# Attention on one core: pair 1 handled by head, score buffers in one PSUM tile, five double-width exponentials, and the order of the work as a table

## The chip, the cores and the metric

The kernel runs on one core of one Trainium2 chip. The metric is device time in microseconds (us); lower is better. A core has a matrix engine (TensorE, PE in the profile; its weight loads are PEld), VectorE (DVE), ScalarE (ACT), GpSimd (POOL) and SyncE (SP), which here only issues transfers. Each engine works through its own queue in order, and a queue waits on semaphores that the others raise. Matrix results land in PSUM, which TensorE writes and VectorE and ScalarE read; everything else lies in SBUF.

## The reference

```python
scores = np.einsum('bhqd,bhkd->bhqk', q, k) * scale       # scale = 1/8
attn = np.exp(scores - scores.max(axis=-1, keepdims=True))
attn = attn / attn.sum(axis=-1, keepdims=True)
return np.einsum('bhqk,bhkd->bhqd', attn, v)
```

q, k and v are float32 of shape 8 x 8 x 512 x 64: 64 heads of 512 positions and 64 features.

## The kernel before

The 64 heads make 32 **pairs** g of two heads (h = 0, 1, called a and b). SyncE loads k, q and v of a pair in 256 KB each (line 509). GpSimd rounds them to float16 (casts: k and q at line 525, v at line 515). TensorE turns k and q so that features lie on partitions (line 558, eight 128x128 transposes for a pair), and VectorE copies the result from PSUM to SBUF (`tqk`, line 571). Scores come transposed, keys on partitions: a **block** is 128 keys by 512 queries, and two blocks make a **group** m, one PSUM buffer of 1024 columns and two banks (`st`). There are three such buffers, used in turn, so the scores of group m (line 598) need the reader of group m-3 to be done. A head's features fill 64 partitions, so the two blocks of a group run side by side on the two halves of the array. The groups are numbered 0 to 128; 127 and 128 are two halves of the last one.

112 groups go to ScalarE: one exponential of 1024 columns each (line 602), from `st` to a float16 tile `pt` (24 of them). The other 16, listed in `Plan.ON_DVE`, go to VectorE, which makes the exponential from bits: a **raise** that reads the buffer (line 625), then five **passes** on SBUF: two scalings (lines 642 and 651), a product (659), a scaling (661) and a product (665). Such a group leaves two tiles, `pe` and `pd`, whose sum is the exponential, so TensorE multiplies twice for it. Then the values (line 704): a **unit** is 128 queries of a head, four or more matmuls of 65 columns, the 65th giving the row's sum. Seven units fill a bank of PSUM; VectorE takes the reciprocals (line 671) and multiplies (line 676) into `ring`, from which SyncE stores heads (line 694). Two more PSUM banks (`x0`, `x1`) serve transposes and values in turn.

Pair 0 is written out by hand (`first_pair`, with its exponentials at line 801). Pair 1 comes next: k and q are loaded in 256 KB each, k is rounded by GpSimd whole, q half by VectorE (line 523) and half by GpSimd (line 524), and it is turned and copied in two parts, k of both heads first and then q of both heads (line 565).

The order of everything else is made by `Plan`: it steps through time with a cost for each operation and writes down, for each engine, what comes when (`step_pe`, `step_dve`, `step_pool`, `step_sp`). Scores go ahead of other work on TensorE when two buffers are free or ScalarE is about to run dry. Casts can be tied behind a VectorE instruction (`cast_behind`), because GpSimd and VectorE share a way to SBUF. The end is written apart: head b of the last pair is multiplied in four parts as its last exponentials come (line 720), normalised (lines 733 and 734) and stored (line 740).

Of the kernel before, what the change touches and what calls it, by code (L numbers as in the profile page):

```python
# [17 lines left out]
class Plan:  # L18

    SLOT, EXP, EXP_DONE, EXP_FIXED = 216, 853, 181, 64  # L20
    INTO, OUT_OF = 96, 96
    TRANSPOSE, V_UNIT = 222, 128
    TO_ACT, TO_DVE, TO_PE = 220, 210, 60

    COPY, NORM, RAISE = (601, 690), (50, 133), (1132, 1215)
    RECIPROCAL = 115
    SCALE, PRODUCT, EXTRA = 333, 600, 29
    COPY_1 = (400, 190)
    NORM_COLUMN, PASS_DONE = 67, 115
    PASSES = (SCALE, SCALE, PRODUCT, SCALE, PRODUCT)  # L30
    BITS = 2
    NEEDS = (None, None, 0, 2, 3)
    FIRST_EXP = 5000
    STEP = 5
    CALM, KEEN = 9000, 4
    FIRST_UNIT = 4
    KNOWN, OVER = (13, 15, 18, 20, 22, 24, 27, 42, 50, 61, 69, 97), 6
    ON_DVE = (5, 10, 16, 25, 28, 39, 44, 54, 63, 66, 74, 81, 91, 96, 103, 116)

    LATE_NORM, LATE_COPY, HURRY, SOON, BACKLOG = 700, 1500, 800, 160, 600  # L40
    LATE_MUL, WAIT = 400, 200
    SLACK, AHEAD = 0, 2

    CAST, CAST_PORT, CAST_DONE, TO_POOL = 557, 475, 130, 150
    SCALE_PORT, PRODUCT_PORT, GAP, REACH = 271, 537, 20, 5
    FIRST_LAND, LOAD, STORE, LATENCY, ISSUE = 5200, 752, 376, 2300, 470
    QUEUED, URGENT = 3500, 16
    PAIRED, STORE_ISSUE = 18, 520
    RAW, QK16, NV, NU = 7, 5, 12, 112
    PAIR, DUEK, DUEV, DUEL, PRE = 3300, 3550, 6000, 5000, 0  # L50

    def __init__(self, groups, pairs, first):
        self.groups, self.pairs = groups, pairs
        self.pe, self.act, self.dve = 7000, self.FIRST_EXP, 6300
        self.pool, self.port, self.dma = 4600, 4600, self.FIRST_LAND
        self.m, self.tiled = first, True
        self.read = []
        self.exps = {}
        for m in range(first):
            self.act += self.EXP + self.EXP_FIXED  # L60
            self.exps[m] = self.act + self.EXP_DONE
            self.read.append(self.exps[m])
        self.tq = {0: 5800}
        self.transposed = {0: 5800}
        self.next_t = 1
        self.part_t = 0
        self.banks = [5100, 5800]
        self.todo = [(g, h) for g in range(pairs) for h in range(2)]
        self.last = self.todo.pop()
        self.last_part = 0  # L70
        self.head = None
        self.units = self.FIRST_UNIT
        self.member = {b: m for m, grp in enumerate(groups) for b in grp}
        self.ready = []
        self.passes = []
        self.passed = {}
        self.raised = set()
        self.steps = []
        self.busy_dve = 0
        self.order, self.paired = [], 0  # L80

        late = {grp[0][0] for m, grp in enumerate(groups) if m in self.ON_DVE}
        due = []
        for g in range(pairs):
            scores = 5000 + self.PAIR * g
            if g:
                due += [(scores - self.DUEK, g, "k"), (scores - self.DUEK + 10, g, "q")]
            due.append((scores + self.DUEV + (self.DUEL if g in late else 0), g, "v"))
        self.due = sorted(due)
        self.uncast = list(self.due)  # L90
        self.casts = []
        self.landed, self.cast_done = {}, {}
        self.first_loads = [(g, n) for _, g, n in self.due if g < self.RAW]
        self.first_loads += [(self.RAW, "k"), (self.RAW, "q")]
        for x in self.first_loads:
            self.dma += self.LOAD
            self.landed[x] = self.dma
        self.loads, self.stores, self.stored = [], [], []
        self.sp = 1650 + 470 * len(self.first_loads)

    def note(self, t, *what):
        self.steps.append((t, len(self.steps)) + what)

    def trigger(self, t):

        ops = self.ops
        if not ops or ops[-1][1] <= t - 300:  # L110
            return 1, None
        n = len(ops) - 1
        while (
            n > 0
            and len(ops) - n < self.REACH
            and not ops[n][2]
            and ops[n][0] - ops[n - 1][1] <= self.GAP
        ):
            n -= 1
        if n > 0 and ops[n][0] - ops[n - 1][1] <= self.GAP:  # L120
            n -= 1
        return len(ops) - n, ops[n][1]

    def emit(self, t, back, after):
        _, g, n = self.uncast.pop(0)
        shared = (g, n) == (1, "q")
        self.note(t, "cast", g, n, back if t > self.CALM else 0)
        if not shared:
            self.casts.append((g, n, t if after is None else after + self.TO_POOL))
        if g + self.RAW < self.pairs:  # L130
            self.loads.append((g + self.RAW, n))

    def fits(self, t, soon=0):
        if not self.uncast:
            return False
        _, g, n = self.uncast[0]
        if n != "v" and g >= self.QK16 and self.transposed.get(g - self.QK16, 1e9) > t:
            return False
        return self.landed.get((g, n), 1e9) <= t + soon

    def step_pool(self, t):
        if self.uncast and self.uncast[0][1:] != (1, "q") and not self.casts and self.pool <= t:
            quiet = not self.passes and self.port <= t and not any(x[1] == "raise" for x in self.ready)
            if self.fits(t) and (quiet or self.uncast[0][0] - self.PRE < t):
                self.emit(t, 1, None)
        if self.casts and self.pool <= t and self.port <= t:
            g, n, after = self.casts[0]
            if after <= t and self.landed.get((g, n), 1e9) <= t:
                self.casts.pop(0)
                begin = max(self.pool, self.port, after, self.landed[(g, n)])  # L150
                self.pool = begin + self.CAST
                self.port = begin + self.CAST_PORT
                self.cast_done[(g, n)] = begin + self.CAST + self.CAST_DONE

    def step_sp(self, t):
        if self.sp > t or (self.loads and self.dma > t + self.QUEUED):
            return
        urgent = len(self.stores) > self.URGENT
        if self.loads and not urgent:
            g, n = self.loads[0]  # L160
            if self.cast_done.get((g - self.RAW, n), 1e9) <= t:
                self.loads.pop(0)
                self.note(t, "load", g, n)
                self.dma = max(self.dma, t + self.LATENCY - self.LOAD) + self.LOAD
                self.landed[(g, n)] = self.dma
                self.sp = t + self.ISSUE
                return
        if self.stores and self.stores[0] <= t:
            both = self.both()
            if both and (len(self.stores) < 2 or self.stores[1] > t):  # L170
                return
            heads = 2 if both else 1
            self.note(t, "store", heads)
            self.dma = max(self.dma, t + self.LATENCY - heads * self.STORE) + heads * self.STORE
            for _ in range(heads):
                self.stores.pop(0)
                self.stored.append(self.dma)
            self.paired += heads - 1
            self.sp = t + self.STORE_ISSUE

    def both(self):

        n = len(self.stored)
        g, h, u = self.order[n]
        return (
            self.paired < self.PAIRED
            and g < self.pairs - 2
            and h == 0
            and n + 1 < len(self.order)
            and self.order[n + 1][0] == g  # L190
            and u % self.NU + 8 <= self.NU
        )

    def room(self, t, u):
        heads = (u - self.NU - self.FIRST_UNIT + 3) // 4
        return heads <= 0 or len(self.stored) >= heads and self.stored[heads - 1] <= t

    def free(self, n=0):
        m = self.m + n
        if m >= len(self.groups):  # L200
            return 1e9
        g = self.groups[m][0][0]
        return max(0 if m < 3 else self.read[m - 3], self.tq.get(g, 1e9))

    def for_dve(self, m):
        return m in self.ON_DVE
# [692 lines left out]
```

## Time and profile before

| | us |
|---|---|
| median of 3 runs | 113.66 (113.52 to 114.11) |
| the profiled execution | 113.92 |
| its span, first to last instruction | 112.1 |
| first exponential starts / last one ends | 5.20 / 108.49 |
| ACT busy | 105.5 (94%) |
| PE busy | 103.2 (92%) |
| DVE busy | 100.8 (90%) |
| POOL busy | 65.9 (59%) |

What lies around the span, 1.8 us, is time before the first and after the last instruction. The page also gives the busy share in 40 slices of 2.8 us, the chain of work that ended last, and groups of instructions with their idle time. One thing is needed to read them: an instruction's recorded time goes from its start to its last write, and the next one on the same engine may start before that. So the distance from start to start is what an instruction costs its engine, not the recorded duration, and a small wait can be hidden in the overlap without any idle time being shown.

### The profile page before, as it was taken

The numbers are of one execution on the slowest core, as the hardware profiler recorded it, in microseconds if no ns is written. First come the engines' busy times: TensorE is split into PE (matmuls) and PEld (weight loads), VectorE is DVE, ScalarE is ACT, GpSimd is POOL, SyncE is SP. The second block draws the span as 40 slices with busy tenths as digits, with TensorE's granted clock in tenths as the row PEclk, the third lists the DMA queues.
The fourth block names the chain that finished last, engine by engine and source line by source line (L and its number), as shares of the span: only waits on it lengthen the run. The fifth ranks groups of instructions, "written<-read, shape, count | busy, mean of one in ns | idle before, by whom it ended". The sixth has DMA issues, their size and how long they took to land.

```text
span 112.1 us, 4408 instructions
## 1 busy us (share of the span) xinstructions
PE 103.2 (92%) x1728; PEld 69.4 (62%) x1728; DVE 100.8 (90%) x227; ACT 105.5 (94%) x118; POOL 65.9 (59%) x127
## 2 busy tenths in 40 slices
PE   7978889999799998999989999899999999999980
PEld 7634555766367766658647767577557577675660
DVE  1647999999999999999999999999999999997390
ACT  4599999999999999999999999999999999999970
POOL 2147768549756886495594786876784855600000
PEclk9999999999999999999999999999999999999997
DMA  3999999999999999999999999999999974142354
GB/s 106 276 359 353 345 350 347 355 336 349 345 347 336 341 346 343 354 364 375 370 358 382 350 355 377 354 372 362 343 366 305 349 245 143 52 141 99 97 167 161
DMA packets 35093, 33.84 MB, mean 302 GB/s; under 512 B 2304, under 2 KB 35072, under 8 KB 35072
## 3 DMA queue, kind: packets, MB, share of 16 engines
q1 hardware_dynamic: 34496, 33.04, 90.4%
q10 hardware_dynamic: 576, 0.52, 1.4%
q8 instruction: 13, 0.21, 0.8%
q14 instruction: 8, 0.07, 0.2%
HBM read 25.17 MB, written 8.39 MB: 299 GB/s over the span
## 4 chain that ended last, share of the span: by engine, by line
DVE 39%; PE 24%; DMA 15%; issue 8%; POOL 7%; SPq 3%; ACT 2%; POOLq 0%; ACTq 0%
PE o L704 13%; DMA v<-in_v_dram 10%; PE st L598 8%; DVE pd L625 8%; DVE tqk L571 7%; DVE ring L676 7%; DMA q<-in_q_dram 5%; DVE m L659 4%; POOL qkp L525 4%; DVE pd L665 4%; POOL vp L515 3%; PE tp L558 2%; SPq L509 2%; DVE m L642 2%; DVE pe L651 2%
## 5 line engine op out<-in xcount | busy, mean ns | idle before, releaser
L602 ACT ACTIVATE pt<-st 128x1024 f16<-128x1024 f32 (+1 forms) x110 | 100.3, 1144 | 0.2 <-PE st L598 0.2
L704 PEld LDWEIGHTS <-pt 128*128 128x128 f16 x880 | 38.8, 98 | 12.1 <-issue 10.2
L704 PE MATMUL o<-vp,pt 128*128 128x65 f16 x880 | 45.3, 194 | 0.4 <-POOL vp L515 0.2
L598 PE MATMUL st<-tqk 64*128 64x512 f16 (+1 forms) x250 | 41.7, 380 | 2.6 <-ACT pt L602 1.4
L525 POOL CAST qkp<-k 128x512 f16<-128x512 f32 x31 | 22.2, 717 | 11.3 <-DVE rc L671 5.3
L525 POOL CAST qkp<-q 128x512 f16<-128x512 f32 x30 | 21.7, 725 | 9.0 <-DVE rc L671 5.3
L515 POOL CAST vp<-v 128x512 f16<-128x512 f32 x32 | 21.4, 679 | 9.2 <-PE st L598 2.4
L676 DVE TENSOR_TENSOR ring<-o,rc 128x448 f32<-128x448 f32 (+2 forms) x37 | 22.3, 606 | 0.4
L704 PE MATMUL o<-vp,pe 128*128 128x65 f16 x128 | 21.8, 194 | 0.0
L704 PE MATMUL o<-vp,pd 128*128 128x65 f16 x128 | 21.7, 192 | 0.0
L558 PE MATMUL tp<-ident,qkp 128*128 128x128 f16 x248 | 19.6, 220 | 1.6 <-DVE tqk L571 0.8
L558 PEld LDWEIGHTS <-qkp 128*128 128x128 f16 x248 | 14.4, 97 | 9.9 <-issue 4.6
L571 DVE COPY tqk<-tp 128x1024 f16<-128x1024 f16 x30 | 20.3, 683 | 0.0
L625 DVE TENSOR_SCALAR pd<-st 128x1024 uint16<-128x1024 f32 x16 | 19.5, 1216 | 0.7 <-PE st L598 0.7
L598 PEld LDWEIGHTS <-tqk 64*128 64x128 f16 x250 | 10.7, 93 | 11.8 <-issue 4.6
L704 PEld LDWEIGHTS <-pe 128*128 128x128 f16 x128 | 12.5, 98 | 3.4 <-issue 3.3
L704 PEld LDWEIGHTS <-pd 128*128 128x128 f16 x128 | 12.5, 98 | 0.0
L659 DVE TENSOR_TENSOR m<-m 128x1024 f16<-128x1024 f16 x16 | 11.0, 685 | 0.0
L665 DVE TENSOR_TENSOR pd<-pd,m 128x1024 f16<-128x1024 f16 x16 | 10.9, 684 | 0.0
L671 DVE RECIPROCAL rc<-o 128x7 f32<-128x7 f32 (+2 forms) x37 | 7.4, 199 | 2.6 <-PE o L704 2.4
L661 DVE TENSOR_SCALAR m<-m 128x1024 f16<-128x1024 f16 x16 | 6.7, 418 | 0.1
L651 DVE TENSOR_SCALAR pe<-pd 128x1024 uint16<-128x1024 uint16 x16 | 6.6, 411 | 0.0
(51 smaller groups left out, 34.9 us busy)
## 6 DMA issues: line engine op xcount, KB each, us to landing
v<-in_v_dram SPq DMA_DIRECT2D x32, 256.0 KB, 5.8
k<-in_k_dram SPq DMA_DIRECT2D x31, 256.0 KB, 5.8
q<-in_q_dram SPq DMA_DIRECT2D x31, 256.0 KB, 5.9
out_dram<-ring SPq DMA_DIRECT2D x18, 256.0 KB, 5.5
out_dram<-ring SPq DMA_DIRECT2D x25, 128.0 KB, 2.2
k<-in_k_dram ACTq DMA_DIRECT2D x2, 128.0 KB, 2.8
q<-in_q_dram SPq DMA_DIRECT2D x2, 128.0 KB, 2.6
out_dram<-ring ACTq DMA_DIRECT2D x2, 128.0 KB, 1.9
```

Of the source, the lines that this page charges most:

```text
L515: return nc.gpsimd.tensor_copy(out=vps[g % NV][:, :, :, 0:D], in_=raw[g]["v"][:, :, :, :])
L525: return nc.gpsimd.tensor_copy(out=dst, in_=src[:, :, :, :])
L558: reads[g] = nc.tensor.transpose(tps[g][:, n, i, :], qkp[g][:, n, i, :], ident)
L571: nc.vector.tensor_copy(out=tqk[g][:, :, :], in_=tps.pop(g).rearrange("p n i c -> p n (i c)"))
L598: nc.tensor.matmul(st[:, x, cols], kc, qc[:, cols], start=True, stop=True)
L602: ins = nc.scalar.activation(out=pt[:, :, cols], in_=st[:, :, cols], func=EXP, scale=scale, bias=SHIFT)
L625: nc.vector.tensor_scalar(out=r["pd"][:, :, :], in0=r["st"][:, :, :], scalar1=BITS, scalar2=BIAS, op0=AluOp.mult, op1=AluOp.add,)
L651: ins = nc.vector.tensor_scalar(out=r["pe"][:, :, :], in0=u[:, :, :], scalar1=0x7C00, scalar2=None, op0=AluOp.bitwise_and,)
L659: ins = nc.vector.tensor_tensor(out=m16, in0=m16, in1=m16, op=AluOp.mult)
L665: ins = nc.vector.tensor_tensor(out=u16, in0=u16, in1=m16, op=AluOp.mult)
L676: nc.vector.tensor_tensor(out=ring[:, u % NU : u % NU + n, :], in0=o[:, x : x + n, 0:D], in1=rcs.pop(u)[:, 0:n].broadcast_to([P, n, D]), o ...
L704: nc.tensor.matmul(os[u // 7][:, u % 7, :], part[:, y * P : (y + 1) * P], vps[g % NV][:, h, c, :], start=(n == 0), stop=(n == len(parts) - 1),
```

## The change

1. **Pair 1 by head.** k and q of pair 1 are loaded in four transfers of 128 KB in the order k of a, q of a, k of b, q of b. GpSimd rounds k of each head, VectorE q of each head (`cast_queries`, step D of the table). Head a is turned first (eight transposes of 64 columns) and copied (64 partitions by 1024 columns); then head b, for which both heads are turned again, eight full transposes, of which 64 partitions are copied. Its groups follow by head: a0a1, a2a3, b0b1, b2b3 instead of a0b0, a1b1 and so on. The last pair's go a0b0, a1b1, a2a3, b2b3 instead of a0a1, a2a3, b0b1, b2b3.
2. **One PSUM tile.** The three score buffers are the three thirds of one tile `sts`; group m uses third (m+1) mod 3. The function `at` tells the scheduler which instructions on it touch different thirds, and that two readers need no order.
3. **Five double exponentials.** Groups 20+21, 51+52, 62+63, 87+88 and 99+100 (`JOINED`) are each done by one exponential of 2048 columns, once both are scored. The `pt` tiles become 19 of 1024 and 2 of 2048 columns.
4. **The order as a table.** `Plan` is gone. A string names every step in order (S scores, V a unit of values, T half a pair of transposes, C copy, R raise, N reciprocal, M multiply, K cast, G load, w/W store, small letters the passes), with lists for the heads, casts (and how far behind which VectorE instruction they are tied), loads and banks. There are 16 groups on VectorE as before, but other ones. The numbers of scores, units, raises, passes, reciprocals, multiplies, casts, loads and stores are those of before. TensorE goes from other work to scores 73 times in the order of before and 86 times in the table.

```diff
-    ON_DVE = (5, 10, 16, 25, 28, 39, 44, 54, 63, 66, 74, 81, 91, 96, 103, 116)
+    ON_DVE = (5, 11, 14, 25, 31, 37, 47, 54, 58, 70, 81, 85, 96, 103, 108, 120)
+    JOINED = (20, 51, 62, 87, 99)
+    SINGLES, DOUBLES = 19, 2
+    PAIR_1 = "a0a1 a2a3 b0b1 b2b3"
+    LAST_PAIR = "a0b0 a1b1 a2a3 b2b3"
+    STEPS = (
+        "KDKTDSCTKSSCKSRKTTSKCVaScVVSKNTMbVTdSCSKRKSTKVTSeSVKCSVfTKRSGTKVVVKCGSSNkTGTKMSGhVVSmGVV"
...
+        "RVwVVVKwSVNVaVVMSScwVVVVbVVdSNeVVVKMSSVwVVNVMwVVVVwSNVMwVVVLLwwNLLMFw"
+    )
+            if g == 1 and name in "kq":
+                halves.append((load_tile(g, name), source(src, g)))
+                if len(halves) == 2:
+                    for h in range(2):
+                        for t, rows in halves:
+                            nc.sync.dma_start(out=t[:, h], in_=rows[:, h])
+                continue
...
+        if g == 1:
+            h = "kq".index(name)
+            return nc.gpsimd.tensor_copy(out=rounded(1, "k")[:, h], in_=raw[1]["k"][:, h])
...
+    def cast_queries(h):
+        dve(nc.vector.tensor_copy(out=rounded(1, "q")[:, h], in_=raw[1]["q"][:, h]))
...
+    def head_transposes(h, bank):
+        cols = slice(0, 64 + 64 * h)
+        t = ps_x.tile([P, 2, NI, P], FP16, tag=f"x{bank ^ h}", name=f"tp_1_{h}")
+        for n in (1, 0):
+            for i in range(NI):
+                reads[1] = nc.tensor.transpose(t[cols, n, i, :], qkp[1][:, n, i, cols], ident)
+        flips.append(t)
...
+    sts = ps_st.tile([P, 3, 2, S], FP32, tag="st", name="sts")
+    def banks(m):
+        return sts[:, (m + 1) % 3], (m + 1) % 3
+    def at(ins, *where, tied=False):
+        pe = nc.tensor.engine
+        for other, there, also in touched[-200:]:
+            apart = there.isdisjoint(where) and not also
+            both_read = pe not in (other.engine, ins.ins.engine)
+            if other.engine != ins.ins.engine and (apart or both_read):
+                tc.declare_no_dep(ins.ins, other, reason="other banks")
+        touched.append((ins.ins, set(where), tied))
...
+        if own == 0 or first_of:
             return
-        ins = nc.scalar.activation(
-            out=pt[:, :, cols], in_=st[:, :, cols], func=EXP, scale=scale, bias=SHIFT
-        )
+        if second_of:
+            low, step = min(bank, (bank + 2) % 3), 1 if bank else 2
+            ins = nc.scalar.activation(
+                out=last["two"][:, :, :, :],
+                in_=sts[:, low : low + step + 1 : step],
+                func=EXP,
+                scale=scale,
+                bias=SHIFT,
+            )
+            at(ins, bank, (bank + 2) % 3)
```

More of the change, by code (lines that the diff above doesn't have):

```diff
@@ L1 @@
 import math
+import re
 from contextlib import ExitStack
@@ L477 @@
     raw = {}
+    halves, flips, copied = [], [], []
     qkp = {}
@@ L579, in scores @@
         cols = slice(256 * half, 256 * half + 256) if half >= 0 else slice(0, S)
-        st = ps_st.tile([P, 2, S], FP32, tag="st", name=f"st_{m}")
+        st, bank = banks(m)
+        own = 0 if on_dve and m not in Order.SPLIT else 1 if on_dve else 2
+        first_of, second_of = m in Order.JOINED, m - 1 in Order.JOINED
         if on_dve:
-            tiles = {n: dpool.tile([P, 2, S], U16, tag=n, name=f"{n}_{m}") for n in ("pe", "pd")}
-            raised[m] = {"st": st, **tiles}
-            parts = [tiles[n].bitcast(FP16) for n in ("pe", "pd")]
+            raised[m] = {"st": st, "own": own, "bank": bank}
+        if own == 0:
+            pass
         elif half == 1:
             pt = last["pt"]
-        else:
-            pt = last["pt"] = ppool.tile([P, 2, S], FP16, tag="pt", name=f"pt_{m}")
+        elif first_of:
+            last["two"] = ppool.tile(
+                [P, 2, 2, S], FP16, tag="pt2", name=f"pt_{m}", bufs=Order.DOUBLES
+            )
+            pt = last["two"][:, int(bank == 2)]
+        elif second_of:
+            pt = last["two"][:, int(bank != 0)]
+        else:
+            pt = last["pt"] = ppool.tile(
+                [P, 2, S], FP16, tag="pt", name=f"pt_{m}", bufs=Order.SINGLES
+            )
         for x, (g, c, h) in enumerate(grp):
@@ L727, in last_values @@
                 )
+                for halves in () if late else last["exps"]:
+                    tc.declare_no_dep(ins.ins, halves, reason="other banks")
     def finish():
@@ L820, in first_pair @@
         nc.vector.tensor_copy(out=qt[:, 1, 0:2], in_=pqb[:, 0:2])
-        pts = [ppool.tile([P, 2, S], FP16, tag="pt", name=f"pt_{m}") for m in range(3)]
+        pts = [ppool.tile([P, 2, S], FP16, tag="pt", name=f"pt_{m}", bufs=Order.SINGLES) for m in range(3)]
         for m in range(3):
@@ L835, in first_pair @@
         nc.vector.tensor_copy(out=qt[:, 1, 2:4], in_=pqb[:, 2:4])
-        st2 = ps_st.tile([P, 2, S], FP32, tag="st", name="st_2")
         for n in range(4):
-            busy(st2[:, 0], P)
-        first_scores(st2, 1, 0, 0, S, pts[2], 0, S)
+            at(busy(sts[:, 0, 0], P), 0)
+        first_scores(0, 1, 0, 0, S, pts[2], 0, S)
         first.update(kt=kt, qt=qt)
     with tc.manual_schedule():
-        plan = Plan(groups, NP, 3)
-        steps = plan.run()
+        order = Order()
         first_loads()
-        for g, name in plan.first_loads:
+        for g, name, _ in order.read(order.FIRST):
             load(g, name)
@@ L866 @@
         }
-        for what, *args in steps:
+        for what, *args in order.steps():
             do[what](*args)
```

617 lines of the change are left out of this document (170 added, 447 removed), and 13 rows, old and new, of tables (CASTS, HEADS, LOADS).

## The prediction

> **What bounds the kernel now.** First the page: which engine is full, and when. Its second part gives the busy tenths of 40 slices of 2.8 us.
>
> ```profile
> PE 103.2 (92%) x1728; PEld 69.4 (62%) x1728; DVE 100.8 (90%) x227; ACT 105.5 (94%) x118; POOL 65.9 (59%) x127
> PE   7978889999799998999989999899999999999980
> DVE  1647999999999999999999999999999999997390
> ACT  4599999999999999999999999999999999999970
> ```
>
> Three engines are full from the fourth slice to the 36th, so no share decides anything; ACT is the one that stays full to the end. Next, ScalarE's own timeline (start, time, instruction):
>
> ```profile
> 5.20 0.60 ACT L801 ACTIVATE pt<-st_0a 128x512 f16<-128x512 f32 x1 [0.43 <-PE st_0a L794]
> 5.69 0.59 ACT L801 ACTIVATE pt<-st_0b 128x512 f16<-128x512 f32 x1
> 6.17 1.95 ACT L801 ACTIVATE pt<-st 128x1024 f16<-128x1024 f32 x2
> 7.98 1.06 ACT L602 ACTIVATE pt<-st 128x1024 f16<-128x1024 f32 x1
> 9.21 99.28 ACT L602 ACTIVATE pt<-st 128x1024 f16<-128x1024 f32 x109 [0.18 <-PE st L598]
> ```
>
> From 9.21 to 108.49 it shows no idle time at all. That is not the whole truth, because one exponential starts before the last one's end is recorded. Two narrow windows of the same timeline give the cost of one when nothing is late:
>
> ```profile
> 56.80 7.60 ACT L602 ACTIVATE pt<-st 128x1024 f16<-128x1024 f32 x8
> ...
> 63.13 3.11 ACT L602 ACTIVATE pt<-st 128x1024 f16<-128x1024 f32 x3
> ```
>
> The second row begins with the eighth exponential of the first: (63.13 - 56.80) / 7 = 0.904 us from start to start. The long row's last exponential has 512 columns and starts at 9.21 + 99.28 - 0.61 = 107.88 (0.61 us is taken from the 0.59 and 0.60 of the first two rows). Between first and last start lie 107 steps of 0.904 and one of 0.49 (5.20 to 5.69), together 97.2 us; they took 98.67. So **1.45 us of waits are hidden** in the body, and 7.98 to 9.21 is 0.33 longer than 0.904. ScalarE loses 1.8 us in all, and this is what the change can win, plus what it saves inside ScalarE.
>
> What makes it wait? The table by stretch (length; PE, PEld, DVE, ACT, POOL busy; clock; DMA share; GB/s) and two rows of the waits (total, times, longest):
>
> ```profile
> 20.00:100.00 80.00, 77.50 (x1333) 52.13 (x1331) 79.68 (x167) 80.00 (x88) 55.08 (x104) 1.00 1.00 328
> 100.00:108.50 8.50, 8.21 (x173) 5.88 (x173) 5.86 (x16) 8.49 (x11) 0.00 (x0) 1.00 0.29 94
> 9.00:108.50 99.50, 95.79 (x1638) 64.22 (x1634) 96.04 (x200) 99.31 (x110) 63.01 (x117) 1.00 0.95 310
> ```
>
> ```profile
> POOL qkp L525 <- DMA k<-in_k_dram: 3.2, 2, 3.0
> ...
> DVE rc L671 <- PE o L704: 2.4, 2, 1.5
> ```
>
> VectorE has 0.3 us free between 20 and 100 us and 2.6 after it, 2.4 of them spent waiting for values. It is a second bound in the middle, with its slack at the wrong end.
>
> **Part by part. The start.**
>
> ```profile
> 6.65 0.62 POOL L525 CAST qkp<-k 128x512 f16<-128x512 f32 x1 [2.98 <-DMA k<-in_k_dram]
> 8.15 0.62 POOL L525 CAST qkp<-k 128x512 f16<-128x512 f32 x1 [0.23 <-DMA k<-in_k_dram]
> 7.37 0.29 DVE L523 CAST qkp<-q 128x256 f16<-128x256 f32 x1 [1.15 <-DMA q<-in_q_dram]
> 7.76 0.97 DVE L565 COPY tqk<-tp 128x512 f16<-128x512 f16 x2
> 8.78 0.39 PE L598 MATMUL st<-tqk 64*128 64x512 f16 x2 [0.52 <-DVE tqk L565]
> ```
>
> k of pair 1 lands at 6.65, q at 7.37, k of pair 2 at 8.15: 0.75 us per 256 KB, so 0.37 per half, and by head they land near 6.28, 6.65, 7.02 and 7.40. VectorE's queue then holds q of a, q of b, copy of a. The second rounding waits for 7.40 and ends by 7.69 (0.29); the copy, at the 0.60 us of a 1024-column copy (row below) and the 0.08 that its record outlasts it, is done near 8.37 instead of 8.73. Scores then end at 8.37 + 0.05 + 0.39 = 8.81, before ScalarE is free at 7.98 + 0.90 = 8.88. The gap of 0.33 goes; bounds 0 (halves land no sooner) and -0.33; I take **-0.30**. SyncE issues two transfers more, 0.5 us each, ahead of the later loads; these are issued some 5 us before they land, which hides it. If that cover is gone, v of pair 0 and the first values are late. VectorE gets 0.6 us more (one rounding, 0.24; two copies of 0.60 for two of 0.40), in a stretch where it waited 1.15 for q. TensorE gets eight transposes more, 0.45.
>
> **The double exponentials.** Two halves cost 0.49 and 0.48 from start to start (5.20, 5.69, 6.17), a whole 0.904. So an instruction's fixed part is 0.06 to 0.08 us, and five fewer save 0.28 to 0.38; I take **-0.30**. *The Trainium skill, ScalarE: Activation LUTs, "What ACT_TABLE_LOAD costs", gives 186 ns beside the columns with immediates, of which 93 overlap: 93 ns each, by which the five would save 0.47, an estimate that these rows do not bear out.* Against it, a double one needs both buffers scored, and its second buffer comes free only when the exponential before the last has ended. The chain of waits shows that path near the end, and a narrow window of ScalarE's timeline the next start:
>
> ```profile
> 103.66 2.02 ACT pt L602 x2
> 105.69 0.04 issue
> 105.73 0.38 PE st L598 x2
> ```
>
> ```profile
> 105.57 1.03 ACT L602 ACTIVATE pt<-st 128x1024 f16<-128x1024 f32 x1
> ```
>
> The buffer's reader ends at 105.69, scores end at 106.11, and ScalarE, which started its next at 105.57, is free at 106.47. So 0.3 us is left, twice per double (the buffers that it frees are refilled in the same way). Bounds: nothing to, with TensorE elsewhere, the whole 0.42 ten times. I take nothing, because the table puts the two scores next to each other or behind a few units.
>
> **The order: VectorE.** The chain of waits gives the cost of each kind:
>
> ```profile
> 27.61 1.14 DVE pd L625
> 28.74 0.60 DVE tqk L571
> 29.34 0.11 DVE rc L671
> 29.45 0.29 DVE m L642
> 29.74 0.53 DVE ring L676
> 30.28 0.33 DVE pe L651
> 30.61 0.60 DVE m L659
> ```
>
> I laid VectorE's queue end to end up to the raise of group 103, which both orders have. Before: 14 raises x 1.13, 39 scalings x 0.33, 26 products and 27 copies x 0.60, 26 reciprocals x 0.11, 26 multiplies x 0.53: 77.2 us, beside 89 groups for ScalarE, 80.5 us. Table: 13 raises, 38 scalings, 25 products, 28 copies, 26 and 26, two roundings: 76.2 us, beside 90 groups less the doubles' 0.30, 81.1. VectorE's room grows from 3.3 to 4.9 us: 1.6 us of its work goes to the end, where it had 2.6 idle. That is as much as the 1.45 hidden in the body.
>
> **The order: TensorE.** This speaks against the change.
>
> ```profile
> 31.86 1.36 PE o L704 x38
> 33.23 0.54 PE st L598 x4
> ...
> 35.71 0.42 PE o L704 x10
> 36.13 0.32 PE st L598 x2
> 36.45 0.55 PE tp L558 x8
> ```
>
> 28 more value matmuls take 0.94: 0.034 each, and 0.08 for entering. A score pair is 0.22 and entering 0.10. Each trip to scores and back costs 0.18; the table makes 86 for 73, 2.3 us more. *The Trainium skill, TensorEngine Tiling (Array Packing), "Key Properties", says that changing the tiling mode drains TensorE; scores use half-height tiles and values do not, and the 0.10 and 0.08 agree.* All of TensorE's work: 1152 value matmuls 38.7, 31 x 8 transposes at 0.45 (0.55 less the entry) 14.0, 125 pairs 27.5, 73 trips 13.1: 93.3 of the 99.5 us from 9.0 to 108.5. After: 93.3 + 2.3 + 0.45 = 96.1 of about 98.3. The idle share falls from 6.2 to 2.2 us, and a queue in order needs some of it. By the profile's own busy time (95.79) it would be 3.7 and nothing. So of the 1.45, between all gone and 2.5 more (next part), I let VectorE's room win **-0.55**.
>
> GpSimd (63 of 99.5 us) and the transfers move the same bytes; the transfers' share is 1.00 to 100 us, yet of GpSimd's 3.2 us of waits for k 3.0 are one wait, at the start. Fewer `pt` tiles cost nothing: in TensorE's queue each is read out ahead of the scores that refill it. I count the dependences of the one tile at nothing as well.
>
> **Sum.** -0.30 - 0.30 - 0.55 = -1.15. On the profiled execution, 113.92 (span 112.1 and 1.8 around it), this is 112.8; that execution lies 0.26 above the median of 113.66, so the forecast is **112.5**.
>
> **Rivals.**
> 1. *The stalls stay.* The body still loses 1.45, because TensorE's trips use up what VectorE gains, or double exponentials start late. For it: the 2.2 us left. Against: VectorE's room. Time: 113.66 - 0.60 = 113.1, or 113.7 if the doubles lose what they save and the start brings half.
> 2. *TensorE becomes the bound*, slower. The 13 trips and eight transposes, 2.8 us, lie in a queue whose 6.2 us of idle time is waiting that must stay. With nothing given up the end moves by 2.8 - 0.3: 116.2. It is slower by over 0.5% if less than 1.9 of the 6.2 can be given up; with 1.0 given up, 115.2. For it: TensorE's 9s in the page. Against: ScalarE's idle time shows PE as releaser only for 0.18 us after the start.
> 3. *The one tile is not kept apart by thirds*, and scores wait for the exponential just before. Then every group shows 0.04 + 0.38 + 0.04 us (8.78 + 0.39 to 9.21) between two exponentials, 110 x 0.46 = 51: 164 us. `at` is written against it.
>
> **Chances.** Forecast 0.62, rival 1 0.19, rival 2 0.16, rival 3 0.03. The low end takes every term's far end: -0.33 - 0.38 - 1.45, 111.5, made 111.6. The high end takes in rival 1 and the mild part of rival 2, where 1.9 us is given up: 114.3. About 0.5% is what a measurement can tell from no change, 113.1 to 114.2. Faster by more than that: the forecast but for a tail of 0.04, and a little of rival 1, 0.61. Within: 0.21. Slower: rivals 2 and 3 less the mild end, 0.18.
>
> **What would show it.** Start: the second row of group exponentials at 8.9 instead of 9.21. Doubles: rows of 128x2048 with a next start 1.75 us later (2 x 0.904 - 0.06); over 1.8 and the wait path is right. Order: 16 raises with VectorE's waits for values at the end below 2.4 us, and ScalarE's first to last start under 101 us. PE: idle time of ACT with releaser PE of over 1 us would be rival 2. The forecast is wrong if the starts of exponentials drift from 0.904 in the middle as they do now.

## The result and the profile after

The changed kernel takes 115.02 us (median of 4 runs, 114.69 to 115.32), beside 113.64 for the kernel before on the same chip: a ratio of 1.0118, 95% interval 1.009 to 1.0146. It is 1.2% or some 1.35 us slower; 112.5 was forecast, and the time lies outside the range of 111.6 to 114.3. The execution that was profiled took 114.69, the fastest of the four, while that of before took 113.92. So the two traces show only about half of the difference, and where a few tenths matter the medians are used.

The page of the kernel after, busy time and tenths:

```profile
PE 105.8 (94%) x1736; PEld 70.6 (63%) x1736; DVE 103.1 (91%) x228; ACT 105.8 (94%) x113; POOL 65.3 (58%) x127
...
PE   7999799989999999999999999999999999999970
...
DVE  1679999999999999999999996999999999999980
ACT  4599999999999999999999999999999999999950
```

PE has become as busy as ACT, 105.8 us each, and from the tenth slice to the 38th its row holds nothing but nines. ScalarE's timeline of the kernel after (start, time, instruction, count):

```profile
5.21 2.92 ACT L574 ACTIVATE pt<-sts 128x512 f16<-128x512 f32 x4 [0.40 <-PE sts L566]
7.99 5.68 ACT L361 ACTIVATE pt<-sts 128x1024 f16<-128x1024 f32 x6
13.87 7.53 ACT L361 ACTIVATE pt<-sts 128x1024 f16<-128x1024 f32 x8 [0.20 <-PE sts L345]
21.35 1.88 ACT L352 ACTIVATE pt<-sts 128x2048 f16<-128x2048 f32 x1
23.12 23.15 ACT L361 ACTIVATE pt<-sts 128x1024 f16<-128x1024 f32 x25
46.03 2.01 ACT L352 ACTIVATE pt<-sts 128x2048 f16<-128x2048 f32 x1
47.90 6.58 ACT L361 ACTIVATE pt<-sts 128x1024 f16<-128x1024 f32 x7
54.34 1.91 ACT L352 ACTIVATE pt<-sts 128x2048 f16<-128x2048 f32 x1
56.10 18.52 ACT L361 ACTIVATE pt<-sts 128x1024 f16<-128x1024 f32 x20
74.41 1.98 ACT L352 ACTIVATE pt<-sts 128x2048 f16<-128x2048 f32 x1
76.19 8.45 ACT L361 ACTIVATE pt<-sts 128x1024 f16<-128x1024 f32 x9
84.52 1.89 ACT L352 ACTIVATE pt<-sts 128x2048 f16<-128x2048 f32 x1
86.30 22.60 ACT L361 ACTIVATE pt<-sts 128x1024 f16<-128x1024 f32 x25
```

Three readings. **The gap at the start is gone**: the row at 7.99 runs on without idle time, where before waited from 7.98 to 9.21. But that gap was no regular part of the kernel before. Six of the runs below start from that kernel and keep pair 1 whole, and none of their traces has it. The one with nine load buffers does the same work at the start, and its ScalarE runs on from the first group to the last:

```profile
8.23 100.67 ACT L602 ACTIVATE pt<-st 128x1024 f16<-128x1024 f32 x110
```

Besides, the change loses as much a little later: its row at 13.87 starts 0.33 late (the start before it was at 12.63, and 12.63 + 0.904 = 13.54). **A double costs 1.76 to 1.78 us** from its start to the next (21.35 to 23.12, 54.34 to 56.10, 74.41 to 76.19, 84.52 to 86.30), against 2 x 0.904; one took 1.87 and holds a wait. **The body waits more.** The last exponential, of 512 columns, starts at 86.30 + 22.60 - 0.61 = 108.29, so 100.30 us lie between the first start of the row at 7.99 and the last one. The instructions need 98 x 0.904 + 0.49 + 5 x 1.76 = 97.88, so 2.42 us are waits. In before the same stretch, from 7.98 to 107.88, held 99.90 for 98.12, so 1.78, of which 0.33 was the start. In the body 1.45 us of waits became 2.4. One trace is good to a few tenths only: the same sum gives 1.4 and 1.9 for two runs below in the order of before (one tile, nine load buffers), and 2.1 to 2.7 for three in the order of the table (three tiles, no doubles, nine load buffers).

The table by stretch of the kernel after, columns as before (length; PE, PEld, DVE, ACT, POOL busy; clock; DMA share; GB/s), and two rows of its waits:

```profile
20.00:100.00 80.00, 78.34 (x1315) 52.13 (x1312) 78.39 (x163) 79.89 (x83) 53.58 (x102) 1.00 1.00 325
100.00:108.50 8.50, 8.50 (x186) 6.41 (x185) 7.88 (x18) 8.50 (x11) 1.64 (x2) 1.00 0.44 146
9.00:108.50 99.50, 97.00 (x1617) 64.08 (x1616) 97.08 (x198) 99.19 (x105) 62.67 (x117) 1.00 0.96 312
```

```profile
POOL vp L221 <- DMA v<-in_v_dram: 3.6, 1, 3.6
...
DVE rc L442 <- PE o L475: 0.7, 3, 0.3
```

VectorE's part came as forecast: from 20 to 100 us it has 1.6 us free where it had 0.3, and at the end it waits 0.7 for values where it waited 2.4. TensorE's room went the other way: 3.7 us of idle time between 9 and 108.5 became 2.5, and after 100 us there is none. The chain of waits of the kernel after runs through TensorE alone there, until VectorE normalises the last values:

```profile
103.64 0.54 PE sts L345 x4
104.18 0.90 PE o L475 x25
105.08 0.32 PE sts L345 x2
105.40 0.58 PE o L475 x15
105.98 0.45 PE sts L345 x3
106.43 0.02 issue
106.45 1.49 PE o L475 x40
107.94 0.32 PE sts L345 x2
108.26 0.63 PE o L475 x16
...
108.91 0.19 DVE rc L442
...
109.13 0.42 DVE ring L447
...
109.68 0.42 DVE obl L506
```

The same place in the chain of before:

```profile
109.10 0.42 DVE obl L734
```

So not all of the loss lies in ScalarE's waits. Of the 0.8 us between the two spans (112.9 and 112.1), 0.41 has come by the end of the last exponential (108.90 and 108.49). In the table VectorE still has another unit's reciprocal and multiply to do when the last values are there: the last multiply (`obl`) ends 1.20 us after the last exponential, where in before it ends 1.03 after it. The remaining 0.2 us is the time to the end of the last store, which differs by as much between runs with the same order.

One cost at the start was not in the prediction. TensorE's timeline of the kernel after:

```profile
8.05 1.63 PE L345 MATMUL sts<-tqk 64*128 64x512 f16 x6
...
10.17 0.60 PE L345 MATMUL sts<-tqk 64*128 64x512 f16 x2
...
11.02 0.39 PE L345 MATMUL sts<-tqk 64*128 64x512 f16 x2
```

TensorE's timeline of before has for the same six matmuls:

```profile
8.78 0.82 PE L598 MATMUL st<-tqk 64*128 64x512 f16 x6 [0.52 <-DVE tqk L565]
```

The score matmuls of pair 1's first three groups took 0.82 in before; here they take 1.63. By head, the two blocks of a group come from the same 64 partitions, that is from the same half of the array, so they run one after the other: 0.60 for two where a group of two heads takes 0.39. Three groups at 0.21 are 0.64 of the 0.81 more; the other 0.17 is a wait for the copy of head b. All four groups at 0.21 are 0.84 us, beside the 0.45 for the second set of transposes. *The Trainium skill, TensorEngine Tiling (Array Packing), "Key Properties", says that different tiles can work in parallel; 0.39 beside 0.60 agrees, and shows what the same tile twice costs.*

### The profile page after: what moved, and what is told of

Its sections match the earlier page's. It is cut to its first block, busy times and chain, and to the rows that moved or that the text cites. A ratio compares the mean times of both kernels' runs of the same rounds, so it can differ in the third digit from the quotient of the medians.

```text
span 112.9 us, 4387 instructions
## 1 busy us (share of the span) xinstructions
PE 105.8 (94%) x1736; PEld 70.6 (63%) x1736; DVE 103.1 (91%) x228; ACT 105.8 (94%) x113; POOL 65.3 (58%) x127
## 4 chain that ended last, share of the span: by engine, by line
DVE 56%; PE 28%; DMA 6%; POOL 4%; issue 3%; SPq 1%; ACT 0%; POOLq 0%
PE o L475 13%; DVE pd L392 11%; DVE tqk L290 11%; DVE ring L447 10%; PE sts L345 9%; DVE pd L436 7%; DMA q<-in_q_dram 6%; DVE m L430 5%; DVE m L432 4%; DVE pe L422 3%; PE tp L265 3%; DVE m L413 3%; POOL qkp L228 3%; DVE rc L442 2%; POOL vp L221 1%
## 5 line engine op out<-in xcount | busy, mean ns | idle before, releaser
L361 ACT ACTIVATE pt<-sts 128x1024 f16<-128x1024 f32 (+1 forms) x100 | 92.4, 1060 | 0.3 <-PE sts L345 0.2
L475 PEld LDWEIGHTS <-pt 128*128 128x128 f16 x880 | 40.1, 98 | 17.8 <-issue 14.1
L475 PE MATMUL o<-vp,pt 128*128 128x65 f16 x880 | 49.2, 195 | 0.9 <-DVE ring L447 0.8
L345 PE MATMUL sts<-tqk 64*128 64x512 f16 (+1 forms) x250 | 43.7, 381 | 1.1 <-ACT pt L361 0.4
L221 POOL CAST vp<-v 128x512 f16<-128x512 f32 x32 | 23.4, 736 | 12.9 <-DMA v<-in_v_dram 3.6
L228 POOL CAST qkp<-q 128x512 f16<-128x512 f32 x30 | 19.6, 658 | 7.6 <-PE sts L345 1.9
L392 DVE TENSOR_SCALAR pd<-sts 128x1024 uint16<-128x1024 f32 x16 | 19.5, 1216 | 0.3 <-PE sts L345 0.3
L345 PEld LDWEIGHTS <-tqk 64*128 64x128 f16 x250 | 11.4, 93 | 10.2 <-issue 2.0
L352 ACT ACTIVATE pt<-sts 128x2048 f16<-128x2048 f32 x5 | 9.7, 1932 | 0.0
L413 DVE TENSOR_SCALAR m<-pd 128x1024 uint16<-128x1024 uint16 x16 | 6.7, 416 | 0.0
```

The lines of the kernel that those rows point to most:

```text
L221: return nc.gpsimd.tensor_copy(out=vps[g % NV][:, :, :, 0:D], in_=raw[g]["v"][:, :, :, :])
L228: return nc.gpsimd.tensor_copy(out=dst, in_=src[:, :, :, :])
L345: at(nc.tensor.matmul(st[:, x, cols], kc, qc[:, cols], start=True, stop=True), bank)
L361: ins = nc.scalar.activation(out=pt[:, 0:own, cols], in_=st[:, 0:own, cols], func=EXP, scale=scale, bias=SHIFT)
L392: ins = nc.vector.tensor_scalar(out=r["pd"][:, own:2, :], in0=r["st"][:, own:2, :], scalar1=BITS, scalar2=BIAS, op0=AluOp.mult, op1=AluOp.add,
L413: ins = nc.vector.tensor_scalar(out=r["m"][:, own:2, :], in0=u[:, own:2, :], scalar1=0x03FF, scalar2=0x3C00, op0=AluOp.bitwise_and, op1=Al ...
```

## The experiments

The theory after the result: TensorE's queue is too full for the scores to come in time. Its rivals: one of the parts does it by itself (one tile, doubles, pair 1 by head), the trips between scores and values, the loads, or single places in the order. Ratios are to the kernel before on the same chip.

### The parts one by one

**The order of before, with pair 1 by head and one tile**, without doubles (shown against the changed kernel):

```diff
-    ON_DVE = (5, 11, 14, 25, 31, 37, 47, 54, 58, 70, 81, 85, 96, 103, 108, 120)
-    JOINED = (20, 51, 62, 87, 99)
-    LAST_PAIR = "a0b0 a1b1 a2a3 b2b3"
+    ON_DVE = (5, 10, 16, 25, 28, 39, 44, 54, 63, 66, 74, 81, 91, 96, 103, 116)
+    JOINED = ()
+    LAST_PAIR = "a0a1 a2a3 b0b1 b2b3"
...
+class Plan:
```

> All parts of the change except the order and the doubles: pair 1 by head, one PSUM tile, single exponentials, but the order, the 16 raised groups and the last pair's groups of before. If the order is what costs (TensorE late), the start's 0.33 us is won and nothing else moves: 113.2 to 113.5. If the new parts cost by themselves (the one tile's dependences, or pair 1 whose two blocks of a group now lie on the same half of the array), it stays near the changed kernel: 114.6 to 115.3.

116.41, ratio 1.0211 (1.0163 to 1.0258): slower even than the whole change. With pair 1 by head, the order of the table is thus better than that of before by some 1%; it repairs part of what the parts cost.

**The whole change without doubles:**

```diff
-    JOINED = (20, 51, 62, 87, 99)
-    SINGLES, DOUBLES = 19, 2
+    JOINED = ()
+    SINGLES, DOUBLES = 24, 2
```

> The changed kernel with five pairs of single exponentials in place of the five doubles (24 tiles of 1024 columns). If the doubles are neutral (they save 5 x 0.05 us in ScalarE and cost about as much in waits before or behind them), the time is that of the changed kernel within 0.3 us: 114.7 to 115.3. If waiting for two scored buffers is what costs, it falls by 1 us or more, to 114 or below.

115.08, 1.0096 (1.0067 to 1.0124). The doubles neither win nor lose anything that can be measured in the total.

**The same with three tiles** of two banks each:

```diff
-    ps_st = ctx.enter_context(tc.tile_pool(name="ps_st", bufs=1, space=bass.MemoryType.PSUM))
+    ps_st = ctx.enter_context(tc.tile_pool(name="ps_st", bufs=3, space=bass.MemoryType.PSUM))
...
-    sts = ps_st.tile([P, 3, 2, S], FP32, tag="st", name="sts")
```

> The same as the kernel without doubles, with three PSUM tiles in turn instead of one tile in thirds. If the one tile only keeps the same dependences, the same time within 0.2 us. If the one tile adds waits between thirds, it is faster than the kernel without doubles by 0.5 us or more.

114.75, 1.0055 (1.0021 to 1.0089). The intervals of the two overlap, so this does not decide whether one tile costs anything in the table. Without both the doubles and the one tile, the table is 0.7 us faster than the whole change by the ratios (1.0055 beside 1.0118). The next run decides for the order of before.

**One tile alone, in the kernel before:**

```diff
+    sts = ps_st.tile([P, 3, 2, S], FP32, tag="st", name="sts")
...
+    def banks(m):
+        return sts[:, (m + 1) % 3], (m + 1) % 3
...
-        st = ps_st.tile([P, 2, S], FP32, tag="st", name=f"st_{m}")
+        st, bank = banks(m)
```

> The kernel before with one thing changed: its three score buffers are the thirds of one PSUM tile. Order, raised groups, pair 1 and exponentials are those of before. If the tile only keeps the same dependences: before within 0.3 us, 113.4 to 114.1. If it adds waits, it carries a good part of the 2.4 us by which e1_order_of_before was slower: 115 or more.

113.88, 1.0003 (0.9979 to 1.0026): in the order of before the one tile costs nothing that can be measured. This run and the next also take over helper functions of the changed kernel, so these cost nothing either.

**Pair 1 by head alone, in the kernel before:**

```diff
+    PAIR_1 = "a0a1 a2a3 b0b1 b2b3"
...
+            if g == 1 and name in "kq":
...
+    def head_transposes(h, bank):
```

> The kernel before with one thing changed: pair 1 is loaded, rounded, turned, copied and scored by head. VectorE gets 0.64 us more at the start, TensorE 0.45 us of transposes and 4 x 0.22 us of scores that no longer run side by side. If these push the full queues behind for good, the time rises by 0.6 to 2.4 us (114.3 to 116.1), and the start gap goes all the same. If they fit into free time, the start's 0.33 us is won: 113.3.

116.13, 1.0198 (1.015 to 1.0247): of the parts tried in the order of before, this is the one that costs, 2.2 us. But that order does not use the head that is ready first. TensorE's timeline has all sixteen transposes in one block ahead of the first scores of pair 1:

```profile
7.22 1.19 PE L597 MATMUL tp<-ident,qkp 128*64 128x128 f16 x16
```

**The whole change with pair 1 whole:**

```diff
-    PAIR_1 = "a0a1 a2a3 b0b1 b2b3"
+    PAIR_1 = "a0b0 a1b1 a2b2 a3b3"
...
+            if what == "cast queries" or what == "copy" and args[0] == 1:
+                continue
```

> The changed kernel with pair 1 as before: whole loads, k by GpSimd, q half and half, copies of k and q, groups a0b0, a1b1 and so on; table, doubles and one tile stay. It takes 0.64 us from VectorE and 1.3 us from TensorE at the start, and gives the start gap of 0.33 us back. If pair 1 by head costs in any order what it cost in the order of before (2.2 us), the time falls to 113 to 113.6; if the table was made for it and holds its room, it stays at 114.7 to 115.3.

114.39, 1.0054 (1.0027 to 1.0081), where the whole change has 1.0118. So pair 1 by head costs the table 0.7 us by the ratios (0.5 if the change is taken at the 1.0095 that it has with nine load buffers, below). The other 0.6 us (1.0054) is there without it, and belongs to the order, the doubles or the one tile.

### TensorE's amount of work

Three kernels leave out the 128 value matmuls with `pe` (a VectorE group then adds only its `pd`, so their output lacks a part). By 0.034 each that is 4.4 us of TensorE's work; everything else stands where it stood.

```diff
-        parts = [(c, part) for c in range(NI) for part in blocks[(g, c, h)]]
+        parts = [(c, part) for c in range(NI) for part in blocks[(g, c, h)][-1:]]
```

The whole change, lighter:

> The changed kernel without the value matmuls of one of the two tiles that a raised group leaves (128 fewer, 4.3 us of TensorE work less; the part of the exponential that they add is missing from the output). If TensorE is what makes ScalarE wait, the waits of the body fall to 1 us or less and the time by 1 to 2 us, to 113.0 to 114.0. If VectorE is, the time stays at 114.5 or more.

The kernel before, lighter:

> The same left out of the kernel before. If its hidden waits come from VectorE's full queue, as the prediction said, it gains less than the changed kernel does: 0 to 0.8 us, 112.9 to 113.7. If they come from TensorE it gains 1 us or more.

The change with pair 1 whole, lighter:

> The changed kernel with pair 1 whole and without the value matmuls of one of the two tiles of a raised group (the part of the exponential that they add is missing from the output). If pair 1 (0.7 us) and TensorE's amount of work (1.1 us) are separate and account for the rise, it comes to the light kernel before, 113.4 to 113.9, or under it by the doubles' 0.25. If they are the same thing, it stays at the light changed kernel, 114.3 to 114.6.

114.48, 1.0024 (0.9993 to 1.0056); 113.72, 0.9984 (0.9958 to 1.0011); and 114.23, 1.0027 (0.9997 to 1.0058). By the ratios the same relief is worth 1.1 us to the change (1.0118 to 1.0024), 0.2 to the kernel before, and 0.3 to the table with pair 1 whole; only the first is clear of nothing, with intervals of some 0.3 us to either side of each ratio. Once TensorE is relieved, pair 1 by head costs nothing that can be measured (1.0024 beside 1.0027), which points to TensorE's time as its price. The stretch of the whole change made lighter, ScalarE's first and last rows, and its exponentials of 512 columns:

```profile
9.00:108.50 99.50, 95.87 (x1501) 61.86 (x1500) 97.38 (x199) 99.45 (x105) 62.91 (x116) 1.00 0.95 310
```

```profile
8.38 13.33 ACT L361 ACTIVATE pt<-sts 128x1024 f16<-128x1024 f32 x14
...
86.40 22.41 ACT L361 ACTIVATE pt<-sts 128x1024 f16<-128x1024 f32 x25
```

```profile
L361 ACT ACTIVATE pt<-sts 128x512 f16<-128x512 f32 x2 | 1.3, 782 | 0.0
```

The last exponential took 0.78 here. From 8.38 to 86.40 + 22.41 - 0.78 = 108.03 are 99.65 us for the same 97.88: 1.77 us of waits instead of 2.42. The traces with pair 1 whole show the same fall, from 2.41 to 1.79, so that pair 1 by head gains more from the relief is seen in the medians and not in the traces. Note PE's busy time: 4.4 us of work less, and only 97.00 - 95.87 = 1.13 less is shown as busy. The rest does not appear as idle time, since a value matmul's record of 195 ns covers a short wait before the next one, which starts some 34 ns after it when nothing is late. So neither a busy share of 94% nor its nines told how much room TensorE had; leaving work out did.

### The trips between scores and values

**The kernel before with more trips** (94): scores are put ahead earlier.

```diff
-    LATE_NORM, LATE_COPY, HURRY, SOON, BACKLOG = 700, 1500, 800, 160, 600
+    LATE_NORM, LATE_COPY, HURRY, SOON, BACKLOG = 700, 1500, 1200, 160, 600
```

> The kernel before with one constant of its planner raised (HURRY 800 to 1200), so that scores are put out one group at a time more often: 94 trips to scores instead of 73, the same work otherwise. If trips are what makes TensorE late, 21 trips of 0.18 us = 3.8 us of TensorE work take most of its free 6.2 us and the time rises by 0.8 to 2 us, to 114.5 to 115.7. If trips fit into idle time, 113.5 to 113.9.

**The table with fewer trips** (73): the scores of 13 groups put off to the next ones.

```diff
+    HELD = (7, 15, 19, 30, 34, 36, 40, 53, 69, 73, 77, 83, 107)
...
+            if what == "scores":
+                if held:
+                    scores(*held)
+                held = args if args[0] in Order.HELD else None
+                if held:
+                    continue
```

> The changed kernel with 13 groups' scores put off until just ahead of the next group's, past one or two units or half a pair of transposes, so that TensorE makes 73 trips to scores as before instead of 86. If the 13 trips (2.3 us of TensorE) are what fills its queue, the time falls by 0.5 to 1.2 us, to 113.8 to 114.5. If only the order of the work around them counts, it stays at 114.8 or rises, because 13 groups are scored later.

**The kernel before with 13 trips more** (86): the second of two adjacent scores goes behind one unit of values.

```diff
+        LATE = (9, 21, 35, 37, 45, 52, 60, 62, 82, 94, 110, 114, 120)
...
+            if what == "scores" and args[0] in LATE:
+                held = args
+                continue
...
+            if held and what == "values":
+                scores(*held)
```

> The kernel before with the second of two adjacent groups' scores moved behind one unit of values, in 13 places: 86 trips to scores instead of 73, nothing else changed. If 13 trips cost as in the table, the time rises by 0.5 to 1.2 us, to 114.2 to 114.9. If TensorE's free time takes them, it stays within 0.3 us.

120.87, 1.0604 (1.0566 to 1.0642), far more than was expected; 117.13, 1.0305 (1.0257 to 1.0353); 115.74, 1.0169 (1.0132 to 1.0206). More trips cost, but fewer cost as well, so this family does not give the price of a trip: each of the three also moves scores. In the one with fewer, ScalarE's timeline shows a new wait where one was put off:

```profile
47.20 1.98 ACT L353 ACTIVATE pt<-sts 128x2048 f16<-128x2048 f32 x1
49.55 1.02 ACT L362 ACTIVATE pt<-sts 128x1024 f16<-128x1024 f32 x1 [0.37 <-PE sts L346]
```

From the start of this double to the next is 2.35 instead of 1.76, 0.59 late, for group 53. The theory that the 13 trips are the loss fell here.

### The places where the scores come late

If a late score is the trouble, it can be done earlier. This moves scores in front of one to three other steps of TensorE: in the table, those of 14 groups ahead of which ScalarE had waited; in the table with pair 1 whole, the same; in the kernel before, four.

```diff
+def advance(steps, ahead):
...
-        for what, *args in order.steps():
+        for what, *args in advance(order.steps(), {13: 2, 21: 1, 28: 1, 53: 2, 57: 1, 69: 2, 73: 1, 98: 1, 105: 1, 109: 1, 110: 3, 122: 1, 123: 2, 128: 3}):
```

```diff
-        for what, *args in steps:
+        for what, *args in advance(steps, {61: 1, 87: 2, 113: 2, 125: 2}):
```

> The changed kernel with the scores of 14 late groups (13, 21, 28, 53, 57, 69, 73, 98, 105, 109, 110, 122, 123, 128) one to three steps of TensorE earlier in the table, 86 trips as in the table. If the place in the queue makes ScalarE wait, most of the 1.4 us that these groups lose goes: 113.7 to 114.3. If TensorE simply has too much to do, the waits come back at other groups: 114.8 to 115.3.

> The same 14 moves in the changed kernel with pair 1 whole. If pair 1 by head costs 0.7 us in the table too, as the kernel with pair 1 whole showed, and the two effects add up: 113.1 to 113.7, the time of before or a little less. If they do not add up, the better of the two alone, about 114.3.

> The kernel before with the scores of groups 61, 87, 113 and 125 one or two steps earlier: the four places where its buffer had been free for over 1.2 us. They lose 0.27 us together: if place is what counts, 113.3 to 113.6; if TensorE then waits for buffers at those places and other work comes late, 113.9 or more.

117.52, 1.0326 (1.0288 to 1.0364); 116.73, 1.0271 (1.0229 to 1.0313); 115.29, 1.013 (1.0088 to 1.0172). All three are slower than the kernels that they start from: the waits go elsewhere. A window of the first one's timeline:

```profile
94.31 0.21 DVE L466 RECIPROCAL rc<-o 128x7 f32<-128x7 f32 x1 [1.26 <-PE o L499]
...
94.58 0.70 POOL L252 CAST qkp<-k 128x512 f16<-128x512 f32 x1 [2.21 <-DMA out_dram<-ring]
94.73 0.62 DVE L471 TENSOR_TENSOR ring<-o,rc 128x448 f32<-128x448 f32 x1
...
95.49 0.61 PE L289 MATMUL tp<-ident,qkp 128*128 128x128 f16 x8 [0.77 <-DVE ring L471]
...
97.34 1.02 ACT L385 ACTIVATE pt<-sts 128x1024 f16<-128x1024 f32 x1 [1.00 <-PE sts L369]
```

The scores that come late here, at 96.85, are those of group 113, which was not moved; those of 109 and 110, which were, stand ahead at 92.08 and 92.77. VectorE's reciprocal waits 1.26 us for values, GpSimd's cast comes late, TensorE's transposes wait 0.77 us for VectorE's multiply, and ScalarE waits 1.00. So in this place what was put ahead made the values, and with them the multiplies that empty their bank, later.

### Loads and casts

**Nine load buffers** instead of seven, in the change and in the kernel before:

```diff
-            bufs=7,
+            bufs=9,
```

> The changed kernel with 9 buffers instead of 7 for each of k, q and v in float32, order as in the table: a load no longer waits for the cast of the pair seven earlier. If late loads are what the table loses by, 113.7 to 114.4; if not, 114.7 to 115.3.

> The kernel before with 9 load buffers. Its casts wait only 0.8 us for loads, so little is to be won: 113.3 to 113.9. If the earlier loads crowd the stores or other loads, 114.2 or more.

115.0, 1.0095 (1.0063 to 1.0126), and 114.02, 1.0011 (0.9966 to 1.0055). The change with nine buffers is as slow as with seven. Loads are not the loss, though GpSimd once waits 3.6 us for v in the change (the row of its waits above).

**The change without the casts' ties** to VectorE's instructions:

```diff
-        if behind:
+        if False:
             tc.add_manual_dep(ins.ins, trail[-behind].ins.name, SYNC, reason="SBUF ports")
```

> The changed kernel without the ties of casts to VectorE instructions, which keep data apart for speed only: casts start as soon as their data is there. If the ties hold casts back where TensorE then waits for them, the time falls to 114.4 or less. If the ties keep casts out of VectorE's passes, it rises by 0.5 to 2 us, because VectorE's passes take longer.

124.17, 1.087 (1.0791 to 1.0948). VectorE's groups without the ties (line, operation, count, busy, mean ns), then with them, in the kernel after:

```profile
L430 DVE TENSOR_TENSOR m<-m 128x1024 f16<-128x1024 f16 x16 | 13.3, 838 | 0.0
...
L432 DVE TENSOR_SCALAR m<-m 128x1024 f16<-128x1024 f16 x16 | 9.4, 587 | 0.0
L413 DVE TENSOR_SCALAR m<-pd 128x1024 uint16<-128x1024 uint16 x16 | 8.8, 548 | 0.0
```

```profile
L430 DVE TENSOR_TENSOR m<-m 128x1024 f16<-128x1024 f16 x16 | 11.1, 702 | 0.0
...
L432 DVE TENSOR_SCALAR m<-m 128x1024 f16<-128x1024 f16 x16 | 6.7, 417 | 0.0
L413 DVE TENSOR_SCALAR m<-pd 128x1024 uint16<-128x1024 uint16 x16 | 6.7, 416 | 0.0
```

Without the ties the kernel loses 9 us, where 0.5 to 2 were expected. VectorE's five passes together take 9.4 us longer (three of them are shown). A little of this is in the change as it stands too, since the products of before are shorter, by the same table of its trace:

```profile
L659 DVE TENSOR_TENSOR m<-m 128x1024 f16<-128x1024 f16 x16 | 11.0, 685 | 0.0
```

(702 - 685) x 16 is 0.27 us for this line.

## Why the prediction was wrong

- **The start** was read from one execution. -0.30 was said, and the gap of 0.33 is gone in the trace; but the traces of six other kernels that come from before, with pair 1 whole, do not have it, so there was little to win, and that the two traces agree with the forecast is luck. Its price was left out as well. "TensorE gets eight transposes more, 0.45" missed the 0.84 us of scores that no longer run side by side. By the same 0.21, LAST_PAIR gives half of that back, but only at the end.
- **The doubles** were right in kind: 0.06 to 0.08 us for an instruction's fixed part was said, 0.03 to 0.05 came (1.76 to 1.78 against 1.808), some 0.2 in all instead of 0.30, and none of it is seen in the total. *The 93 ns that the prediction took from the Trainium skill, ScalarE: Activation LUTs, "What ACT_TABLE_LOAD costs", are about twice that or more; the Trainium skill, Perfetto Trace Analysis, "Optimizing Scalar/DVE Operations", has about 51 ns for Scalar on PSUM; the upper end of these rows, 0.05 us, agrees with it.*
- **One tile at nothing** was right in the order of before (1.0003) and is not settled for the table. Rival 3, at 164 us, is dead.
- **VectorE's room** came as counted (0.3 to 1.6 us between 20 and 100, the wait at the end 2.4 to 0.7). The step that failed is the next one, "I let VectorE's room win **-0.55**". The room did not end the waits; the body's waits grew, by about 1.0 us in the two traces, because what ScalarE waits for is TensorE.
- **TensorE** was weighed and priced too low. The idle share was said to fall "from 6.2 to 2.2 us", and rival 2 was given 0.16. With the scores one after another TensorE gets 0.84 more at the start than was counted. Rival 2, with 1.0 us given up, said 115.2; 115.02 was measured. It had the right engine, but the near figure is luck, since 1.0 was one value of many and the 0.84 was not in its sum. The runs with less for TensorE show that it is this engine: by the ratios 1.1 of the 1.35 us come back with 128 matmuls gone (0.8 if the 1.0095 of the change with nine load buffers is taken for its level), where the kernel before gains 0.2. Most of the loss is thus TensorE's. ScalarE's idle time shows PE for 0.2 us only, so the sign that the prediction named for rival 2 (over 1 us) was the wrong place to look: these waits are hidden in the overlap.
- **What each part costs depends on the order**: pair 1 by head 2.2 us in the order of before and 0.5 to 0.7 in the table.

What stays open is 0.4%: lightened, the change stands at 1.0024 and the kernel before at 0.9984, 0.45 us apart with intervals that just overlap. Of this, 0.1 is seen after the last exponential: from its end to that of the last multiply are 1.13 us in the lighter change and 1.03 in the kernel before made lighter. The one tile in the table is another candidate. No run took work from VectorE, to which pair 1 by head adds 0.6 us at the start, so its share is not told apart. Casts that meet VectorE's products (702 beside 685 ns) would go that way, but that is argued and no run shows it. Nor is the price of a single trip settled, since every run that changed their number also moved scores in time.

## What to carry to other kernels

Where three engines are over 90% full, a part that saves a wait at one place must be charged with everything it adds to each engine, work that no longer runs side by side included. To learn whether an engine is the bound, leave some of its work out: a busy share or a named releaser does not say it. An order that was tuned as a whole is not mended in single places: of the runs that moved scores, all six became slower than the kernel that they started from. And a wait in one trace is worth counting only if it is there in the next one.

## What the runs showed of the hardware

- Casts on GpSimd that run beside VectorE's passes on SBUF lengthen these: 416 ns became 548, 417 became 587 and 702 became 838 in the mean. The price here is 9 us of 115. *The Trainium skill, SBUF — State Buffer, "Who interferes with whom", says that when VectorE in a two-port mode meets GpSimd, whichever issues first has the shared ports for the whole instruction; the longer passes agree with it in kind.*
- Taking 4.4 us of matmuls out lowered TensorE's recorded busy time by 1.1 us only.
